# HGRN2 recurrence of a hybrid streaming encoder: keys as logarithms in the exponent, a sigmoid without a reciprocal, merged predicated copies

## The chip, the cores and the metric

The kernel runs on one core of a Trainium2 chip. The metric is the device time of one execution in microseconds (us). Three runs of the kernel before the change gave 1269.4, 1276.73 and 1278.02 us; their median is 1276.73 us.

## The reference

The input x has 2048 tokens of 1024 channels. One layer normalises it, projects it once to 3592 columns, and gives these to three branches whose outputs are gated, joined and projected back. Branch A is the HGRN2 recurrence in four heads of 64 channels, and it is the one that the change touches:

```python
z = f_a
f_gate = lb + (1.0 - lb) * sigmoid(z)
log_f_a = log(maximum(f_gate, TINY))
k_a = (1.0 - lb) * sigmoid(-z)
q = silu(q_a)
...
# by chunk, b = cumsum(log_f) within the chunk, S the 64x64 state of a head
decay = exp(b[t] - b[s]) for s <= t, else 0
attn[t, s] = sum_d q[t, d] * k[s, d] * decay[t, s, d]
o = attn @ v + (q * exp(b)) @ S
S = exp(b_last)[:, None] * S + (k * exp(b_last - b)).T @ v
```

Branch B is a pooling mixer, branch C a forgetting attention with 8 heads. Both need the projections and the attention takes most of the time, but no instruction of theirs changes.

## The kernel before, in words

All matmuls that need more than half precision are done with halves: weights and normalised x are each split in a float16 high and low part, and a projection is three products (24 matmuls of 512 columns for one 128-channel block of 512 tokens). The recurrence itself computes in float32; one float32 matmul stands as two records in the trace.

The work of the recurrence is cut in eight units (g, ct): four groups g of 512 tokens, two blocks ct of 128 channels (two heads, one on partitions 0 to 63, one on 64 to 127). A unit has three pieces.

- hgrn_f projects the forget gate and makes from it, channel by channel, log sigmoid (sg), the key k, the logarithm of the gate (E), its running sum b (a scan on VectorE, L275), and from these the scaled keys and queries: Kd and Qd for the diagonal, khat for the state, qhat for reading the state.
- hgrn_q projects the query and multiplies it with its sigmoid. The sigmoid is 1/(1 + exp(-q)): an Exp on ScalarE (L303), a clamp and an addition (L304) and a reciprocal (L305) on VectorE; the product is qs (L307), which goes into Qd and qhat on GpSimd (VectorE for g = 0).
- hgrn_unit builds the causal 128 x 128 score block of each of four 128-token chunks and two heads in the tile `at`, then multiplies it with the values. The diagonal blocks of two tokens come from pd = Kd.T Qd (L326), one head after the other, masked into `at` by L327. The rest comes in six levels, h = 64, 32, ..., 2: the second half of a block of 2h tokens sees the first half through the value of b at the middle. For each level GpSimd writes two differences into a tile X (L345, L346), ScalarE takes Exp of it (L347), VectorE multiplies the first halves with k (L351) and writes the second halves times qs into a tile Z (L354, once for each head), TensorE makes pl = X.T Z (L358), and VectorE copies pl under a mask into `at`, once for each head (L363). At the second level the states S are carried over the four chunks on VectorE (L378), at the fourth po begins with the state's part (L383), and after the sixth it takes `at` times the values (L390).

The tile X has four buffers, Z three. The eight units follow each other in a loop. In the turn of a unit the features of the next unit (hgrn_f, hgrn_q) are made as well, and the function fill puts other work of TensorE between the levels: projections of the values (L196), of the attention's keys (L185), and the loading and transposing of further x tiles. Each engine has one queue of its own in order; the tile framework decides at build time, by its estimates, in which order the instructions of these pieces stand in each queue. From the last units on, kq_chunk and kq_blocks follow with the attention's projections; they load weights through a staging tile wst with three buffers, split into halves by ScalarE (L163) and VectorE (L166). After the recurrence come the projections, the pooling and the attention.

Of the kernel before, what the change touches and what calls it, by code (L numbers as in the profile page):

```python
# [54 lines left out]
def kernel(  # L55
# [30 lines left out]
    # f_c side: persistent small tables  # L86
# [6 lines left out]
    # DRAM scratch  # L93
# [22 lines left out]
    # normalised x transposed, hi and lo, in two halves of the tokens  # L116
# [61 lines left out]
    def proj_cm(ps, w, c0, g):  # L178
        """channel-major: ps[128 ch, 512 tokens of group g]"""
# [8 lines left out]
    def proj_tm(ps, w, c0, n, t):  # L188
        """token-major: ps[128 tokens of tile t, n channels]"""
# [60 lines left out]
    def hgrn_f(g, ct, wf, bank=None):  # L250
# [10 lines left out]
        # log sigmoid of z and of -z  # L261
# [14 lines left out]
        # blocks of two tokens refer to their first token  # L276
# [10 lines left out]
        G.tensor_tensor(kk.rearrange("p (n t) -> p n t", t=P), bt[:, :, P - 1:P].to_broadcast([P, 4, P]), bt, op=ALU.subtract)  # L287
        S.activation(kk, kk, AF.Exp, bias=0.0, scale=1.0)
        G.tensor_tensor(kk, kk, k, op=ALU.mult)
# [4 lines left out]
        feats[(g, ct)] = dict(k=k, b=b, qd=q_d, kd=k_d, kk=kk, qh=e, el=el)  # L294

    def hgrn_q(g, ct, wq):
# [7 lines left out]
        V.tensor_scalar(th, th, 1e37, 1.0, op0=ALU.min, op1=ALU.add)  # L304
        V.reciprocal(th, th)  # L305
# [10 lines left out]
    def hgrn_unit(g, ct, va):  # L316
        f = feats.pop((g, ct))
        k, b, qs = f["k"], f["b"], f["qs"]
        u = f"_{g}_{ct}"
        at = ap.tile([P, 2, 4, P], F32, tag="at", name=f"at{u}", bufs=2)  # L320
        for hh in range(2):
            r = ds(64 * hh, 64)
            pd = pm(f"pd{u}_{hh}")
            for tt in range(4):
                tok = ds(tt * P, P)
                PE.matmul(pd[:, tok], f["kd"][r, tok], f["qd"][r, tok], start=tt == 0, stop=tt == 3, skip_group_check=True)  # L326
            V.tensor_tensor(at[:, hh], pd.rearrange("p (t s) -> p t s", t=4),  # L327
                            mdiag.unsqueeze(1).to_broadcast([P, 4, P]), op=ALU.mult)
# [6 lines left out]
        # levels of halves: the second half of a block sees its first half through the middle  # L335
        for li, h in enumerate(LEVELS):
# [3 lines left out]
            bv = b.rearrange("p (n two h) -> p n two h", two=2, h=h)  # L340
            Xv = X.rearrange("p (n two h) -> p n two h", two=2, h=h)
# [843 lines left out]
```

## Time and profile before

| | us |
|---|---|
| three runs | 1269.4, 1276.73, 1278.02 |
| median | 1276.73 |
| span of the profiled execution, first to last instruction | 1271.3 |
| median less that span | 5.4 |
| TensorE (PE) busy in the span | 1188.4 |
| VectorE (DVE) busy | 843.6 |
| ScalarE (ACT) busy | 604.2 |
| GpSimd (POOL) busy | 413.5 |

The own time of the profiled execution is not among the files beyond its span; what lies around the span is taken as the 5.4 us that the median has more. The recurrence lies between some 45 us, where the first unit's features are made, and 364 us, where the last unit's output is done.

A busy TensorE is one whose matmul records cover the time; the end of a record is modelled and successive records overlap. "PEclk" is the granted share of its clock. Times of instructions that follow each other on one engine overlap by some tens of nanoseconds too, so a sum of durations is a little more than the time that they cover.

### The profile page before, as it was taken

The numbers are of one execution on the slowest core, as the hardware profiler recorded it, in microseconds if no ns is written. First come the engines' busy times: TensorE is split into PE (matmuls) and PEld (weight loads), VectorE is DVE, ScalarE is ACT, GpSimd is POOL, SyncE is SP. The second block draws the span as 40 slices with busy tenths as digits, with TensorE's granted clock in tenths as the row PEclk, the third lists the DMA queues.
The fourth block names the chain that finished last, engine by engine and source line by source line (L and its number), as shares of the span: only waits on it lengthen the run. The fifth ranks groups of instructions, "written<-read, shape, count | busy, mean of one in ns | idle before, by whom it ended". The sixth has DMA issues, their size and how long they took to land. (4 is left out here: it accounts for less than half of the span.)

```text
span 1271.3 us, 25715 instructions
## 1 busy us (share of the span) xinstructions
PE 1188.4 (93%) x10077; PEld 767.6 (60%) x10077; DVE 843.6 (66%) x1703; ACT 604.2 (48%) x1167; POOL 413.5 (33%) x516
## 2 busy tenths in 40 slices
PE   5878999998999999999999999999999899999998
PEld 3445766655654478885447776765555555555644
DVE  5799888888542244213354798788888898888522
ACT  5745544443221133212122667667667676777611
POOL 2646466554230011001240223234333343334400
PEclk9989999998999999999999999999999999999999
DMA  9636320112146233001012253275222332221253
GB/s 226 165 84 140 77 42 26 43 34 83 47 121 167 77 113 97 11 24 42 18 34 88 77 145 105 63 162 125 81 71 69 85 76 78 48 50 51 70 165 106
DMA packets 168139, 107.57 MB, mean 85 GB/s; under 512 B 95825, under 2 KB 159569, under 8 KB 168017
## 3 DMA queue, kind: packets, MB, share of 16 engines
q1 hardware_dynamic: 166976, 105.92, 31.9%
q8 instruction: 79, 1.29, 0.5%
q14 instruction: 44, 0.35, 0.1%
q10 hardware_dynamic: 1040, 0.00, 0.0%
HBM read 59.62 MB, written 31.59 MB: 72 GB/s over the span
## 5 line engine op out<-in xcount | busy, mean ns | idle before, releaser
L1001 ACT ACTIVATE pf<-st,biasg 128x512 f32<-128x512 f32 (+1 forms) x320 | 199.6, 625 | 101.1 <-PE st L992 59.1
L961 DVE TENSOR_REDUCE M<-mx 128x1 f32<-128x512 f32 (+3 forms) x288 | 173.4, 615 | 18.6 <-PE mx L957 12.0
L196 PEld LDWEIGHTS <-hTh 128*128 128x128 f16 x1536 | 151.1, 99 | 44.9 <-DMA hTh<-xh 15.6
L1006 DVE TENSOR_TENSOR pl<-pf,ph 128x512 f16<-128x512 f32 (+1 forms) x213 | 138.1, 650 | 46.6 <-POOL ph L1003 26.6
L1006 POOL TENSOR_TENSOR pl<-pf,ph 128x512 f16<-128x512 f32 (+2 forms) x107 | 112.7, 1053 | 152.3 <-ACT ph L1005 144.9
L1016 PE MATMUL o<-Vt,ph 128*128 128x65 f16 x1088 | 130.5, 193 | 3.6 <-DVE oc L1030 3.5
L1005 ACT ACTIVATE ph<-st,biasg 128x512 f16<-128x512 f32 (+2 forms) x213 | 131.3, 616 | 1.5 <-PE o L1018 1.5
L1017 PE MATMUL o<-Vt,ph 128*128 128x64 f16 x1088 | 130.9, 195 | 0.0
L1018 PE MATMUL o<-Vt,pl 128*128 128x65 f16 x1088 | 129.8, 192 | 0.0
L1003 POOL TENSOR_SCALAR ph<-pf 128x512 f16<-128x512 f32 (+1 forms) x107 | 65.8, 615 | 195.9 <-ACT pf L1001 124.0
L1016 PEld LDWEIGHTS <-ph 128*128 128x128 f16 x1088 | 103.0, 97 | 35.3 <-DVE oc L1030 5.7
L1017 PEld LDWEIGHTS <-ph 128*128 128x128 f16 x1088 | 102.3, 97 | 24.3 <-issue 0.8
L991 PE MATMUL st<-QQ,K 128*128 128x512 f16 (+1 forms) x320 | 111.4, 348 | 5.1 <-ACT ph L1005 4.3
L1018 PEld LDWEIGHTS <-pl 128*128 128x128 f16 x1088 | 102.7, 99 | 0.4
L1060 PE MATMUL y<-woh,mh 128*128 128x512 f16 (+2 forms) x264 | 98.4, 374 | 0.0
L1060 PE MATMUL y<-woh,ml 128*128 128x512 f16 (+2 forms) x264 | 98.3, 374 | 0.0
L1060 PE MATMUL y<-wol,mh 128*128 128x512 f16 (+2 forms) x264 | 98.3, 374 | 0.0
L957 PE MATMUL mx<-KA,QM 68*128 68x512 f16 (+1 forms) x224 | 79.6, 358 | 4.8 <-DVE M L961 4.0
L196 PEld LDWEIGHTS <-hTl 128*128 128x128 f16 x768 | 76.2, 99 | 10.7
L992 PE MATMUL st<-QB,KA 68*128 68x512 f16 x224 | 80.4, 359 | 0.0
L1060 PEld LDWEIGHTS <-mh 128*128 128x128 f16 x528 | 49.5, 98 | 50.7 <-issue 1.3
L358 PE MATMUL pl<-Z,X 128*128 128x128 f32 x384 | 54.1, 295 | 22.7 <-DVE Z L354 22.7
(327 smaller groups left out, 2738.9 us busy)
## 6 DMA issues: line engine op xcount, KB each, us to landing
xt<-in_x_dram SPq DMA_DIRECT2D x16, 512.0 KB, 4.5
xr<-in_x_dram SPq DMA_DIRECT2D x16, 512.0 KB, 5.0
out_dram<-yt SPq DMA_DIRECT2D x15, 512.0 KB, 3.0
QQ<-qh_d SPq DMA_DIRECT2D x64, 64.0 KB, 2.4
wo<-in_w_out_dram SPq DMA_DIRECT2D x16, 256.0 KB, 3.0
gc_d<-gtc SPq DMA_DIRECT2D x32, 128.0 KB, 2.0
gtl<-gc_d SPq DMA_DIRECT2D x16, 256.0 KB, 3.0
wst_q<-in_w_in_dram SPq DMA_DIRECT2D x12, 256.0 KB, 2.8
```

Of the source, the lines that this page charges most:

```text
L196: PE.matmul(ps, a[:, k, :], b[:, k, c0:c0 + n], start=i == 0, stop=i == 3 * KC - 1)
L957: PE.matmul(mx[:, :w], QMs[i][:68, qi * P:(qi + 1) * P], KA[c][:68, h, :w], start=True, stop=not last)
L961: V.tensor_reduce(dst, mx[:, :w], op=ALU.max, axis=AX.X)
L991: PE.matmul(st[:, off:], K2[c][:, h, jj * P:(jj + 1) * P], QQs[i][:, off:], start=True, stop=False)
L992: PE.matmul(st[:, off:], KA[c][:68, h, jj * P:(jj + 1) * P], QBs[i][:68, off:], start=False, stop=not diag)
L1001: S.activation(pf[:, off:], st[:, off:], AF.Exp, bias=bias, scale=0.125)
L1005: S.activation(ph[:, off:], st[:, off:], AF.Exp, bias=bias, scale=0.125)
L1006: (G if k == 1 else V).tensor_tensor(pl[:, off:], pf[:, off:], ph[:, off:], op=ALU.subtract)
L1016: PE.matmul(pov[:, qi, :], ph[:, qs], Vt[:, j, h, 0:65], start=(j == 0 and qi == 0), stop=False, skip_group_check=True)
L1017: PE.matmul(pov[:, qi, 0:64], ph[:, qs], Vt[:, j, h, 65:129], start=False, stop=False, skip_group_check=True)
L1018: PE.matmul(pov[:, qi, :], pl[:, qs], Vt[:, j, h, 0:65], start=False, stop=(j == 4 * g + qi), skip_group_check=True)
L1060: PE.matmul(py, a[:, k, :], b[:, k, cs], start=i == 0, stop=i == 3 * KC - 1)
```

## The change

The key enters the level's exponent as its logarithm. With log k = log sigmoid(-z) + log(1 - lb), a new tile nb = log k - b is made once for each unit on VectorE (L276 of the changed kernel), and the subtraction of b on the first halves of X becomes an addition of nb, so that the Exp gives the decayed key and the product with k goes. The same is done for khat (the addition of nb on GpSimd, no product) and for Kd (a subtraction of log f from log sigmoid(-z), before the Exp, whose bias is log(1 - lb)). The Exp that gave sigmoid(-z) and the tile k go. The sigmoid of the query becomes exp(-ln(1 + exp(-q))): a clamp on VectorE, then Ln and Exp on ScalarE, in place of the reciprocal. `at` has the chunk ahead of the head in its layout, so that one predicated copy a level serves both heads. The diagonal's matmuls go chunk by chunk, alternating between the heads, into two banks of PSUM. Two small instructions on 128 x 2 elements make log(1 - lb) once.

```diff
@@ hgrn_f
         E1.tensor_tensor(z, sg, z, op=ALU.subtract)
-        S.activation(z, z, AF.Exp, bias=0.0, scale=1.0)
-        k = t512("k", f"k{u}")
-        G.tensor_scalar(k, z, lbt[:, 4 + ct:5 + ct], 1.0, op0=ALU.mult, op1=ALU.mult)
+        lk = lbt[:, 8 + ct:9 + ct]
...
         V.tensor_tensor_scan(b, d0, E, initial=0.0, op0=ALU.mult, op1=ALU.add)
+        nb = t512("nb", f"nb{u}")
+        V.scalar_tensor_tensor(nb, z, lk, b, op0=ALU.add, op1=ALU.subtract)
...
-        S.activation(k_d, lfo, AF.Exp, bias=0.0, scale=-1.0)
+        E1.tensor_tensor(k_d, z, lfo, op=ALU.subtract)
+        S.activation(k_d, k_d, AF.Exp, bias=lk, scale=1.0)
         S.activation(q_d, lfo, AF.Exp, bias=0.0, scale=1.0)
-        E1.tensor_tensor(k_d, k_d, k, op=ALU.mult)
...
-        G.tensor_tensor(kk..., bt[:, :, P - 1:P].to_broadcast([P, 4, P]), bt, op=ALU.subtract)
+        G.tensor_tensor(kk..., bt[:, :, P - 1:P].to_broadcast([P, 4, P]), nb..., op=ALU.add)
         S.activation(kk, kk, AF.Exp, bias=0.0, scale=1.0)
-        G.tensor_tensor(kk, kk, k, op=ALU.mult)
@@ hgrn_q
         S.activation(th, pq, AF.Exp, bias=0.0, scale=-INV)
-        V.tensor_scalar(th, th, 1e37, 1.0, op0=ALU.min, op1=ALU.add)
-        V.reciprocal(th, th)
+        V.tensor_scalar(th, th, 2.0 ** 60, None, op0=ALU.min)
+        S.activation(th, th, AF.Ln, bias=1.0, scale=1.0)
+        S.activation(th, th, AF.Exp, bias=0.0, scale=-1.0)
@@ hgrn_unit
-        at = ap.tile([P, 2, 4, P], F32, tag="at", name=f"at{u}", bufs=2)
-        for hh in range(2):
-            pd = pm(f"pd{u}_{hh}")
-            for tt in range(4):
-                PE.matmul(pd[:, tok], f["kd"][r, tok], f["qd"][r, tok], ...)
+        at = ap.tile([P, 4, 2, P], F32, tag="at", name=f"at{u}", bufs=2)
+        pds = [pm(f"pd{u}_{hh}") for hh in range(2)]
+        for tt in range(4):
+            for hh in range(2):
+                PE.matmul(pds[hh][:, tok], f["kd"][r, tok], f["qd"][r, tok], ...)
...
-            E1.tensor_tensor(Xv[:, :, 0, :], mid, bv[:, :, 0, :], op=ALU.subtract)
+            E1.tensor_tensor(Xv[:, :, 0, :], mid, nbv[:, :, 0, :], op=ALU.add)
             S.activation(X, X, AF.Exp, bias=0.0, scale=1.0)
-            V.tensor_tensor(Xv[:, :, 0, :], Xv[:, :, 0, :], kv[:, :, 0, :], op=ALU.mult)
...
-            for hh in range(2):
-                dst = at[:, hh].rearrange(...)
-                V.copy_predicated(dst, masks[h]....to_broadcast([P, 4, nb, h]), plv[:, :, hh]...)
+            dst = at.rearrange("p t u (n two h) -> p (t u) n two h", two=2, h=h)[:, :, :, 1, :]
+            V.copy_predicated(dst, masks[h]....to_broadcast([P, 8, n2, h]), pl.rearrange("p (u n h) -> p u n h", u=8, h=h))
```

The order of each engine's queue follows from the code and the framework's estimates. On VectorE, in the turn of unit (2, 1) before the change, these rows prepare the next unit (3, 0) and begin the current one; th is the query's sigmoid, el a copy of four columns of qhat:

```order
L273 TENSOR_SCALAR E_0_2338<-E_0_2338,lbt 128x512
L275 SCALAR_TENSOR_TENSOR b_0_2354<-d_391,E_0_2338 128x512
L304 TENSOR_SCALAR th_0_2412<-th_0_2412 128x512
L327 TENSOR_TENSOR at_1_2420<-pd_1_0_2421,mdiag 128x512
L305 RECIPROCAL th_0_2412<-th_0_2412 128x512
L293 COPY el_0_2368<-qhat_0_2366 128x4
L327 TENSOR_TENSOR at_1_2420<-pd_1_1_2427,mdiag 128x512
L307 TENSOR_TENSOR qs_0_2416<-th_0_2412,pq_0_2387 128x512
```

The same place in the changed kernel:

```order
L271 TENSOR_SCALAR E_0_2274<-E_0_2274,lbt 128x512
L273 SCALAR_TENSOR_TENSOR b_0_2287<-d_393,E_0_2274 128x512
L305 TENSOR_SCALAR th_0_2346<-th_0_2346 128x512
L276 SCALAR_TENSOR_TENSOR nb_0_2289<-z_0_2273,lbt,b_0_2287 128x512
L331 TENSOR_TENSOR at_1_2355<-pd_1_0_2356,mdiag 128x4x128
L293 COPY el_0_2302<-qhat_0_2300 128x4
L331 TENSOR_TENSOR at_1_2355<-pd_1_1_2357,mdiag 128x4x128
L309 TENSOR_TENSOR qs_0_2351<-th_0_2346,pq_0_2321 128x512
```

The reciprocal is gone, nb stands where it can run after the scan, and qs, whose input now comes back from ScalarE, stands at the same place. On ScalarE, the same turn before the change has these rows from the query's Exp on:

```order
L303 ACTIVATE th_0_2412<-pq_0_2387 128x512
L282 ACTIVATE Kd_0_2358<-sg_0_2343 128x512
L283 ACTIVATE Qd_0_2357<-sg_0_2343 128x512
L288 ACTIVATE khat_0_2362<-khat_0_2362 128x512
L291 ACTIVATE qhat_0_2366<-b_0_2354 128x512
```

and the changed kernel has these:

```order
L303 ACTIVATE th_0_2346<-pq_0_2321 128x512
L285 ACTIVATE Qd_0_2292<-sg_0_2279 128x512
L291 ACTIVATE qhat_0_2300<-b_0_2287 128x512
L284 ACTIVATE Kd_0_2293<-Kd_0_2293,lbt 128x512
L306 ACTIVATE th_0_2346<-th_0_2346 128x512
L289 ACTIVATE khat_0_2297<-khat_0_2297 128x512
L307 ACTIVATE th_0_2346<-th_0_2346 128x512
```

The Ln and the last Exp of the sigmoid stand behind the Exps of Qd, Kd and khat, whose inputs come from GpSimd. On TensorE, a unit's diagonal before the change (the four matmuls of a head in one row) and the transposes behind it:

```order
L185 MATMUL pq_1_2022<-hTl_102,wh_q 128x512
L326 MATMUL pd_0_0_2056<-Qd_0_1676,Kd_0_1677 128x128 x4
L326 MATMUL pd_0_1_2062<-Qd_0_1676,Kd_0_1677 128x128 x4
L331 MATMUL pk_0_2068<-idf,khat_0_1681 128x128 x4
L196 LDWEIGHTS hTh_101
```

and in the changed kernel:

```order
L185 MATMUL pq_1_1316<-hTl_100,wh_q 128x512
L329 MATMUL pd_0_0_1351<-Qd_0_992,Kd_0_993 128x128
L329 MATMUL pd_0_1_1352<-Qd_0_992,Kd_0_993 128x128
L329 MATMUL pd_0_0_1351<-Qd_0_992,Kd_0_993 128x128
L329 MATMUL pd_0_1_1352<-Qd_0_992,Kd_0_993 128x128
L329 MATMUL pd_0_0_1351<-Qd_0_992,Kd_0_993 128x128
L329 MATMUL pd_0_1_1352<-Qd_0_992,Kd_0_993 128x128
L329 MATMUL pd_0_0_1351<-Qd_0_992,Kd_0_993 128x128
L329 MATMUL pd_0_1_1352<-Qd_0_992,Kd_0_993 128x128
L335 MATMUL pk_0_1363<-idf,khat_0_997 128x128 x4
```

The two heads, on the lower and the upper 64 partitions, alternate; what stands before and behind is the same.

## Rows read from the trace of the kernel before

**Rows 1.** The page: busy us by engine, share of the span, instructions.

```profile
PE 1188.4 (93%) x10077; PEld 767.6 (60%) x10077; DVE 843.6 (66%) x1703; ACT 604.2 (48%) x1167; POOL 413.5 (33%) x516
```

**Rows 2.** Windows from one unit's diagonal to the next: length, busy us, PEclk.

```profile
45.00:62.10 17.10, 16.40 (x100) 9.49 (x98) 15.72 (x20) 13.31 (x25) 12.19 (x20) 1.00 0.38 91
62.10:109.70 47.60, 37.64 (x200) 24.37 (x200) 44.92 (x79) 24.09 (x44) 24.82 (x28) 0.89 0.42 104
109.70:143.50 33.80, 28.60 (x193) 21.82 (x192) 30.25 (x58) 16.75 (x31) 20.11 (x23) 0.90 0.46 96
143.50:181.90 38.40, 34.33 (x245) 26.02 (x244) 32.94 (x58) 19.39 (x37) 24.27 (x26) 0.96 0.29 63
181.90:214.20 32.30, 32.08 (x198) 20.43 (x197) 27.70 (x55) 13.03 (x22) 19.84 (x22) 1.00 0.08 25
214.20:247.20 33.00, 32.47 (x245) 25.04 (x244) 31.24 (x59) 14.57 (x34) 18.18 (x20) 1.00 0.15 41
247.20:282.90 35.70, 32.53 (x197) 20.57 (x196) 31.00 (x60) 16.13 (x30) 21.02 (x23) 1.00 0.10 31
282.90:332.10 49.20, 44.59 (x246) 27.09 (x245) 35.96 (x69) 14.92 (x30) 19.33 (x20) 0.93 0.24 71
332.10:364.50 32.40, 32.40 (x201) 20.81 (x201) 15.61 (x37) 6.12 (x11) 2.44 (x4) 1.00 0.13 43
```

**Rows 3.** Waits, 45 to 366 us: total us, times, longest us.

```profile
POOL X L345 <- PE pl L358: 39.3, 12, 10.3
...
PE pl L358 <- DVE Z L354: 22.7, 11, 5.2
POOL khat L287 <- DVE b L275: 15.8, 4, 8.5
```

**Rows 4.** Timeline around 128 us, DVE then PE: start, us, instruction, idle before.

```profile
124.50 2.46 DVE L378 SCALAR_TENSOR_TENSOR S<-S,el,pu 64x64 f32<-64x64 f32 x8
...
128.35 2.05 PE L358 MATMUL pl<-Z,X 128*128 128x128 f32 x8 [5.20 <-DVE Z L354]
```

**Rows 5.** Groups on DVE, 45 to 366 us: total us, mean ns, idle before.

```profile
L363 DVE COPY_PREDICATED at<-m,pl 128x256 f32<-128x256 int8 x96 | 39.5, 482 | 2.4 <-PE pl L358 2.2
L305 DVE RECIPROCAL th<-th 128x512 f32<-128x512 f32 x8 | 26.7, 3337 | 0.0
L351 DVE TENSOR_TENSOR X<-X,k 128x256 f32<-128x256 f32 x48 | 23.2, 484 | 1.6 <-ACT X L347 0.4
...
L327 DVE TENSOR_TENSOR at<-pd,mdiag 128x512 f32<-128x512 f32 x16 | 10.7, 679 | 0.0
L275 DVE TENSOR_TENSOR_SCAN b<-d,E 128x512 f32<-128x512 f32 x8 | 10.5, 1318 | 0.1
...
L262 DVE SCALAR_TENSOR_TENSOR sg<-z,E 128x512 f32<-128x512 f32 x8 | 5.5, 690 | 4.3 <-ACT E L259 4.2
```

**Rows 6.** Groups on POOL, then on ACT, 45 to 366 us, as above.

```profile
L278 POOL TENSOR_TENSOR sg<-E,odd 128x512 f32<-128x512 f32 x6 | 10.1, 1686 | 10.6 <-DVE E L273 10.6
L287 POOL TENSOR_TENSOR khat<-b 128x512 f32<-128x512 f32 x8 | 9.6, 1196 | 15.8 <-DVE b L275 15.8
...
L284 POOL TENSOR_TENSOR Kd<-Kd,k 128x512 f32<-128x512 f32 x6 | 7.7, 1277 | 0.7 <-ACT Kd L282 0.7
...
L347 ACT ACTIVATE X<-X 128x512 f32<-128x512 f32 x48 | 30.1, 629 | 67.2 <-POOL X L346 63.2 <-DVE at L363 3.0 <-PE pl L358 0.9
```

**Rows 7.** Timeline of PE at 181.9 us and at 189.2 us.

```profile
181.91 1.71 PE L326 MATMUL pd<-Qd,Kd 64*128 64x128 f32 x16
...
189.23 1.95 PE L358 MATMUL pl<-Z,X 128*128 128x128 f32 x16
```

**Rows 8.** Timeline at 300 us, ACT, DVE and PE.

```profile
300.29 0.91 ACT L163 ACTIVATE wh_q<-wst_q,g 128x256 f16<-128x256 f32 x2 [6.97 <-DMA wst_q<-in_w_in_dram]
...
302.66 0.88 DVE L166 SCALAR_TENSOR_TENSOR wl_q<-wst_q,g,wh_q 128x256 f16<-128x256 f32 x2 [0.94 <-ACT wh_q L163]
...
308.92 2.05 PE L358 MATMUL pl<-Z,X 128*128 128x128 f32 x8 [4.61 <-DVE Z L354]
```

More of the change, by code (lines that the diff above doesn't have):

```diff
@@ L293, in hgrn_f @@
         V.tensor_copy(el, e.rearrange("p (n t) -> p n t", t=P)[:, :, P - 1])
-        feats[(g, ct)] = dict(k=k, b=b, qd=q_d, kd=k_d, kk=kk, qh=e, el=el)
+        feats[(g, ct)] = dict(nb=nb, b=b, qd=q_d, kd=k_d, kk=kk, qh=e, el=el)
     def hgrn_q(g, ct, wq):
@@ L317, in hgrn_unit @@
         f = feats.pop((g, ct))
-        k, b, qs = f["k"], f["b"], f["qs"]
+        nb, b, qs = f["nb"], f["b"], f["qs"]
         u = f"_{g}_{ct}"
-        at = ap.tile([P, 2, 4, P], F32, tag="at", name=f"at{u}", bufs=2)
-        for hh in range(2):
-            r = ds(64 * hh, 64)
-            pd = pm(f"pd{u}_{hh}")
-            for tt in range(4):
-                tok = ds(tt * P, P)
-                PE.matmul(pd[:, tok], f["kd"][r, tok], f["qd"][r, tok], start=tt == 0, stop=tt == 3, skip_group_check=True)
-            V.tensor_tensor(at[:, hh], pd.rearrange("p (t s) -> p t s", t=4),
+        at = ap.tile([P, 4, 2, P], F32, tag="at", name=f"at{u}", bufs=2)
+        pds = [pm(f"pd{u}_{hh}") for hh in range(2)]
+        for tt in range(4):
+            tok = ds(tt * P, P)
+            for hh in range(2):
+                r = ds(64 * hh, 64)
+                PE.matmul(pds[hh][:, tok], f["kd"][r, tok], f["qd"][r, tok], start=tt == 0, stop=tt == 3, skip_group_check=True)
+        for hh in range(2):
+            V.tensor_tensor(at[:, :, hh, :], pds[hh].rearrange("p (t s) -> p t s", t=4),
                             mdiag.unsqueeze(1).to_broadcast([P, 4, P]), op=ALU.mult)
@@ L340, in hgrn_unit @@
             bv = b.rearrange("p (n two h) -> p n two h", two=2, h=h)
+            nbv = nb.rearrange("p (n two h) -> p n two h", two=2, h=h)
             Xv = X.rearrange("p (n two h) -> p n two h", two=2, h=h)
@@ L359, in hgrn_unit @@
                           start=tt == 0, stop=tt == 3, skip_group_check=True)
-            nb = 64 // h
-            for hh in range(2):
-                dst = at[:, hh].rearrange("p t (n two h) -> p t n two h", two=2, h=h)[:, :, :, 1, :]
-                V.copy_predicated(dst, masks[h].rearrange("p (n h) -> p n h", h=h).unsqueeze(1).to_broadcast([P, 4, nb, h]),
-                                  plv[:, :, hh].rearrange("p t (n h) -> p t n h", h=h))
+            n2 = 64 // h
+            dst = at.rearrange("p t u (n two h) -> p (t u) n two h", two=2, h=h)[:, :, :, 1, :]
+            V.copy_predicated(dst, masks[h].rearrange("p (n h) -> p n h", h=h).unsqueeze(1).to_broadcast([P, 8, n2, h]),
+                              pl.rearrange("p (u n h) -> p u n h", u=8, h=h))
             if li == 1:
@@ L389, in hgrn_unit @@
                 c = 64 * hh
-                PE.matmul(po[:, tt * P + c:tt * P + c + 64], at[:, hh, tt, :], va[:, tt, ct * P + c:ct * P + c + 64],
+                PE.matmul(po[:, tt * P + c:tt * P + c + 64], at[:, tt, hh, :], va[:, tt, ct * P + c:ct * P + c + 64],
                           start=False, stop=(tt == 3 and hh == 1), skip_group_check=True)
@@ L510 @@
     tok_i(3, wi, toks[0])
-    lbt = ap.tile([P, 8], F32, tag="lbt", name="lbt", bufs=1)
+    lbt = ap.tile([P, 10], F32, tag="lbt", name="lbt", bufs=1)
     nc.sync.dma_start(lbt[:, 0:2], lower_bounds.rearrange("o (c p) -> p (o c)", p=P), allow_slow_non_contiguous=True)
@@ L527 @@
     V.tensor_tensor(lbt[:, 6:8], lb_e, lb_r, op=ALU.add)
+    V.tensor_scalar(lb_e, lbt[:, 4:6], 2.0 ** -50, None, op0=ALU.max)
+    S.activation(lbt[:, 8:10], lb_e, AF.Ln, bias=0.0, scale=1.0)
     wq = load_w([(QA, 256)], "q")
```

3 lines of the change are left out of this document (1 added, 2 removed).

## The prediction

> **What bounds the kernel now.** I read the busy times by engine first. TensorE is busy for 93% of the span, VectorE for 66% [rows 1], so over the whole kernel TensorE is the bound, and a change that takes work from VectorE can win only where TensorE stands idle. The busy share by stage settles where that is. I cut the recurrence at the first diagonal matmul of each unit, so that a window is one turn of its loop [rows 2]; each row gives the window's length, then busy time of PE, weight load, DVE, ACT and POOL, and the granted clock. The reader is to subtract: in nine windows of 319.5 us together, TensorE is busy for 291.0, so 28.5 us of idle time is all that lies there. It sits in the second (10.0), third (5.2), fourth (4.1), seventh (3.2) and eighth (4.6) window and is 0.7 or less in the others. After 332 us TensorE is covered to the last digit. In the second window VectorE is busy for 44.9 of 47.6 us: there VectorE is the bound. In the third, fourth and seventh it has 87 to 90%, close enough that its queue comes late in bursts.
>
> The clock adds something. The granted share is 0.89, 0.90, 0.96 and 0.93 in the four windows with the longest idle stretches and 1.00 elsewhere [rows 2]: in them TensorE fell to 1.2 GHz of its 2.4 after it had stood idle. The missing share times the length is 5.2 + 3.4 + 1.5 + 3.4 = 13.5 us of clock, most of it under work, so some 10 us of work was done late for that.
>
> Then the waits: TensorE's largest wait in this stretch is the first level matmul behind Z, 22.7 us in 11 waits [rows 3]. The timeline shows one such wait, of 5.2 us, with VectorE working all the while: state updates for 2.46 us, then copies, then Z [rows 4]. So most of the idle time is VectorE's queue being late with Z, and VectorE is what the change relieves.
>
> **The change part by part**, for one unit and VectorE first.
>
> - The reciprocal goes: 3.34 us [rows 5].
> - Six products with k go, 6 x 0.484 = 2.9 us [rows 5].
> - Twelve masked copies of 256 columns, 12 x 0.482 = 5.8 us, become six of 512. No row shows such a copy with 512. Not more than two of the old, 0.96; not less than the masked product of 512 columns from PSUM, 0.68 [rows 5], so six cost 4.1 to 5.8 us. A masked copy of 256 costs about what a product of 256 costs, 0.48, so I take near the middle, 5.2: a gain of 0.6.
> - nb is new: a scalar_tensor_tensor on 128 x 512, 0.69 us by its sister on L262 [rows 5].
> - The clamp remains as one instruction on the same tile; the two instructions on 128 x 2 elements come once and are hidden under the weights' split at the start; at worst their cost is a fraction of a us.
>
> Sum: 3.34 + 2.9 + 0.6 - 0.69 = 6.15 us less on VectorE for each unit, 49 us over eight. GpSimd loses a product of 1.3 to 1.4 us and the scaling of k for each unit, and its remaining instructions keep their number; it is at most 63% busy in these windows [rows 2] and hides what it does. ScalarE loses one Exp and gains a Ln and an Exp, 0.63 us net by the Exp of the same size [rows 6]; it is at half load.
>
> A new wait comes with it. The order shows qs at the same place in VectorE's queue, but its sigmoid now ends on ScalarE behind the Exps of Kd and khat, which wait for GpSimd. From E on, GpSimd needs 1.69 + 1.28 + 1.20 = 4.2 us for sg, Kd and khat, and two Exps follow at 0.63 [rows 6]: qs can start about 5.4 us after E. VectorE has the scan, nb, two products for the diagonal, the clamp and el ahead, 1.32 + 0.69 + 2 x 0.68 and about 0.6: 4.0 us [rows 5]. So VectorE stands some 1.5 us at qs, with the masked copies, the state updates and Z of the running unit queued behind it, and TensorE waits for that Z. This may be nothing where E is late anyway, and up to the reciprocal's own 3.3 us where GpSimd is held; I take 1.5 where VectorE bounds, which leaves 4.6 us of a turn.
>
> Diagonal: 16 records take 1.71 us now; 16 records of the level matmuls, which use all 128 partitions, take 1.95 [rows 7]. So the two heads already run side by side for a little, 0.24 us, at the one place where they meet. Alternating can bring between nothing and the time of eight records, 1.71 - 0.98 = 0.7 us a unit. I take 0.4, in the seven windows in which TensorE will be the bound: 2.8 us.
>
> The Trainium skill's page "TensorE: Matmul & The Clock Gate", section "Part 3: Packing small matmuls — row/col tiling", says that matmuls on different row groups of the array run concurrently, at nearly the time of one. By that rule the gain is the whole 0.7 us a unit, 5.6 over eight, and the total would be 3 us below mine; the trace shows only the partial overlap just named.
>
> Now the windows. A window can't be shorter than TensorE's work at full clock, nor than VectorE's.
>
> - First: 0.7 idle, 0.5 of it gained.
> - Second: VectorE bounds before and after, about 40 us against TensorE's 37.6 less the clock's part; it gives the 4.6 of VectorE and about 0.9 because the first b comes before a reciprocal instead of behind it: 5.5.
> - Third: VectorE falls from 30.2 to about 25.6, TensorE has 28.6 with 0.10 of the clock missing, about 26.9; with some waiting left, 29.0 of 33.8: 4.8.
> - Fourth: TensorE about 33 at full clock, VectorE 28; 34.0 of 38.4: 4.4.
> - Fifth and sixth: TensorE is already the bound; 0.4 of 0.75.
> - Seventh: 3.2 idle, VectorE down to 26 of 35.7: 2.3.
> - Eighth: here the late Z hangs on weights as well. ScalarE waits 6.97 us for a weight transfer and VectorE then for ScalarE, before the 4.61 us in which TensorE stands [rows 8]. The transfer starts when VectorE has freed a staging buffer, so it comes earlier by the reciprocal but keeps its own length: half of the 4.6 + 3.4 of idle and clock, 4.0.
> - Ninth: nothing.
>
> Sum: 0.5 + 5.5 + 4.8 + 4.4 + 0.4 + 2.3 + 4.0 = 21.9, with the diagonal 24.7 us. The profiled span of 1271.3 becomes 1246.6. The median of the runs is 5.4 above that span, which I keep: 1276.7 - 24.7 = 1252.0 us. What follows the recurrence stays in order and simply starts earlier, since TensorE has no idle time there in which to lose the gain.
>
> **Rivals.**
>
> 1. TensorE alone bounds. All 28.5 us of idle time, the 10 of the clock and the 2.8 go: 1276.7 - 41.3 = 1235.4. For it: VectorE ends at least 2 us below TensorE in every window but the second. Against it: the second, and the weights in the eighth. Chance 0.17.
> 2. The sigmoid's new way takes the reciprocal's place: VectorE stands at qs for about the 3.3 us that it saves, and only the products and copies, 2.8 us less a unit, count. That is half: 1276.7 - 12.5 = 1264. For it speaks ScalarE's new order, against it that in four windows VectorE has time to stand. Chance 0.13.
> 3. The levels are bound elsewhere, and VectorE was only the last in a chain: ScalarE waits 63.2 us for GpSimd's X [rows 6], GpSimd 39.3 us for TensorE to free X [rows 3]. Then only the shorter chain inside the waits and the diagonal remain, some 4 us: 1273. Against it: GpSimd has a third of each window free. Chance 0.12.
> 4. Slower: VectorE's stop at qs becomes longer than the 6.15 us saved. The place is the turn of each unit, where khat on GpSimd stands behind X of the running unit, X behind TensorE's pl, and pl behind a Z that is queued behind qs. GpSimd's longest waits of this kind are 10.3 us for pl and 8.5 for khat's b [rows 3]. At 8.5 a unit the kernel loses 8 x (8.5 - 6.15) = 19 us: 1296. It decides from 6.15 us of stop on; my estimate is 1.5. Chance 0.08.
>
> The Trainium skill speaks for the fourth in "TensorE: Matmul & The Clock Gate", section "Architectural detail: the array is 16× 32×32, not 1× 128×128": VectorE's and ScalarE's queues are strictly first in, first out, so nothing overtakes a waiting qs. By that rule, the trace agrees: copies and state updates follow VectorE's wait for weights at 302.66 us [rows 8].
>
> **How the numbers follow.** The forecast has a chance of 0.50, with 1245 to 1259 as its own range: 7 us either way for the stop at qs between nothing and 3.3, the copies between 4.1 and 5.8, and the diagonal between nothing and 0.7. With the rivals' 0.17 below, 0.13 and 0.12 above and 0.08 slower, the range of 8 in 10 is 1233 to 1268. A change of over 1% is about 12.8 us, and that is about what a measurement of this kernel tells from none: below 1264 faster, above 1289.5 slower. Faster: 0.50 + 0.17 + nearly three quarters of rival 2, 0.09: 0.76. Same: the rest of rival 2, rival 3 and the mildest of rival 4: 0.18. Slower: 0.06.
>
> **What would show it.** In the changed profile VectorE should be busy some 45 us less up to 364 us, with no reciprocal of 512 columns and 48 masked copies of about 0.87 us. TensorE's waits for Z should fall from 22.7 us to under 10, mostly in the first unit and the last two. VectorE should show a wait for th from ScalarE of 1 to 2 us a unit; 6 us or more there proves the fourth rival, none the first. The diagonal should take about 1.3 us. The last recurrence output should leave some 25 us earlier and the later stages keep their length; if those lengthen, the forecast is wrong in what it left out.

## The result, and the profile after

The changed kernel takes 1258.42 us, the median of four runs from 1256.87 to 1260.66; four runs of the kernel before beside it had a median of 1275.82. The ratio is 0.987, with a 95% interval of 0.9846 to 0.9895: faster by 17.4 us, where the prediction had 24.7. The profiled execution has a span of 1256.6 us and took 1258.33, so 1.7 us lie outside its span; in the runs below it is 1.6 to 2.1. The 5.4 us that stand for this before the change must then be for the most part the distance of a quicker execution from the median. The two spans differ by 14.7 us (1271.3 to 1256.6), and the windows below account for these 14.7, not for the 17.4 of the medians. On its page VectorE is busy 32.1 us less than in [rows 1] (843.6 to 811.5), not 45 less.

The page of the changed kernel, busy us by engine:

```profile
PE 1177.0 (94%) x10077; PEld 758.5 (60%) x10077; DVE 811.5 (65%) x1608; ACT 608.9 (48%) x1176; POOL 398.3 (32%) x500
```

The windows of the changed kernel, cut as in [rows 2] at each unit's first diagonal matmul: length, then busy us of PE, weight load, DVE, ACT and POOL, granted clock, DMA share, GB/s. The last window runs to the end of the last output, which in the kernel before is at 368.4 us.

```profile
45.00:62.20 17.20, 17.20 (x105) 9.94 (x103) 16.04 (x23) 13.24 (x25) 15.56 (x26) 1.00 0.26 64
62.20:106.70 44.50, 36.06 (x198) 22.72 (x197) 36.50 (x60) 24.64 (x45) 15.41 (x19) 0.88 0.49 130
106.70:145.00 38.30, 28.60 (x197) 21.63 (x196) 29.54 (x52) 22.78 (x40) 21.87 (x24) 0.91 0.53 131
145.00:178.65 33.65, 31.97 (x245) 24.48 (x244) 24.46 (x43) 15.39 (x31) 20.38 (x21) 1.00 0.03 9
178.65:210.55 31.90, 31.49 (x197) 19.95 (x196) 25.52 (x43) 13.65 (x23) 18.00 (x19) 1.00 0.08 25
210.55:242.30 31.75, 31.75 (x247) 24.42 (x246) 27.24 (x49) 17.20 (x37) 18.66 (x19) 1.00 0.16 43
242.30:274.20 31.90, 31.50 (x199) 19.94 (x198) 27.20 (x46) 15.42 (x29) 17.18 (x19) 1.00 0.12 34
274.20:319.90 45.70, 43.66 (x245) 25.58 (x244) 31.97 (x56) 16.14 (x31) 18.29 (x19) 0.96 0.27 76
319.90:355.90 36.00, 36.00 (x219) 22.20 (x219) 17.00 (x35) 8.72 (x17) 5.48 (x7) 1.00 0.19 58
```

Set against [rows 2], the second window is 3.1 us shorter, the third 4.5 *longer*, the fourth 4.7 shorter, the seventh 3.8 and the eighth 3.5. The last output of the recurrence leaves 12.5 us earlier (368.4 to 355.9), and what follows it takes 900.8 us instead of 902.9.

One caution on such numbers: the time after the recurrence is the same code in every kernel of this study, and in fourteen profiles it lies between 899.2 and 906.1 us. Two or three microseconds of a single profile's span are no evidence. The medians are, and so are some windows: the sixth and the ninth repeat to 0.3 us in kernels that don't touch them. The seventh does so with the change, but takes 35.6 to 37.3 us in kernels without it that don't touch it.

Waits of the changed kernel, 45 to 356 us (total us, times, longest):

```profile
PE pl L361 <- DVE Z L357: 15.0, 6, 8.4
...
PE pu L370 <- ACT khT L337: 7.6, 3, 4.6
...
DVE xl L222 <- ACT xh L220: 7.1, 5, 1.8
...
ACT xh L215 <- DMA xt<-in_x_dram: 4.9, 2, 3.2
...
DVE ss L216 <- ACT xh L215: 4.0, 2, 3.1
...
DVE qs L309 <- ACT th L307: 1.8, 3, 0.6
```

The wait for Z of [rows 3] fell from 22.7 only to 15.0 us, more than half of it in one piece of 8.4. The stop at qs, which the prediction put at 1.5 us a unit, is 1.8 us in all eight units. A wait for khT, the transposed keys that ScalarE copies from PSUM, is new. New as well are waits for the x tiles (xt, xh, xl and ss belong to the normalisation of x, of which eight tiles pass through these windows): VectorE stands 7.1 + 4.0 us for ScalarE's part of them, and ScalarE 4.9 us for the loading of x. In the kernel before, from 55 to 366 us, VectorE stood 1.3 us for a tile and ScalarE not at all for a load:

```profile
DVE xl L222 <- ACT xh L220: 1.3, 2, 1.0
```

Groups on VectorE in the changed kernel, 45 to 356 us, as [rows 5]:

```profile
L357 DVE TENSOR_TENSOR Z<-X,qs 64x256 f32<-64x256 f32 x96 | 51.6, 537 | 1.5
L365 DVE COPY_PREDICATED at<-m,pl 128x512 f32<-128x512 int8 x48 | 38.7, 806 | 1.3 <-PE pl L361 1.1
...
L273 DVE TENSOR_TENSOR_SCAN b<-d,E 128x512 f32<-128x512 f32 x8 | 12.0, 1498 | 0.1
...
L276 DVE SCALAR_TENSOR_TENSOR nb<-z,lbt,b 128x512 f32<-128x512 f32 x8 | 10.5, 1307 | 0.0
```

nb costs 1.31 us, not 0.69. The 48 merged copies keep VectorE busy for 38.7 us, where the 96 of [rows 5] did for 39.5: the merge saved almost nothing. And the scan costs 1.50 instead of 1.32.

### The profile page after: what moved, and what is told of

The parts are those of the page before. It is cut to its first block, busy times and chain, and to the rows that moved or that the text cites. A ratio compares the mean times of both kernels' runs of the same rounds, so it can differ in the third digit from the quotient of the medians.

```text
span 1256.6 us, 25632 instructions
## 1 busy us (share of the span) xinstructions
PE 1177.0 (94%) x10077; PEld 758.5 (60%) x10077; DVE 811.5 (65%) x1608; ACT 608.9 (48%) x1176; POOL 398.3 (32%) x500
## 3 DMA queue, kind: packets, MB, share of 16 engines
q1 hardware_dynamic: 166976, 105.92, 32.1%
## 5 line engine op out<-in xcount | busy, mean ns | idle before, releaser
L196 PEld LDWEIGHTS <-hTh 128*128 128x128 f16 x1536 | 150.6, 99 | 46.4 <-DMA hTh<-xh 18.6
L196 PE MATMUL pgc<-wh_gc,hTh 128*128 128x256 f16 x256 | 67.3, 275 | 1.2 <-DVE gtb L848 1.2
```

The source lines that it names most:

```text
L196: PE.matmul(ps, a[:, k, :], b[:, k, c0:c0 + n], start=i == 0, stop=i == 3 * KC - 1)
```

## The experiments

Twelve kernels ran, in three sets. "Windows" are cut as above, and each ratio is to runs of the kernel before on the same chip.

### First set: which part pays

Theory A: relief of VectorE is worth about what it takes off, except in the first units, which the x tiles and the khT copy hold. Theory B: the sigmoid on ScalarE gave back what the reciprocal's removal won.

**Keys as logarithms alone.** The kernel before with the edit's key half, and sigmoid, copies and diagonal as they were:

```diff
-        S.activation(z, z, AF.Exp, bias=0.0, scale=1.0)
...
-        G.tensor_scalar(k, z, lbt[:, 4 + ct:5 + ct], 1.0, op0=ALU.mult, op1=ALU.mult)
...
+        V.scalar_tensor_tensor(nb, z, lk, b, op0=ALU.add, op1=ALU.subtract)
...
-            V.tensor_tensor(Xv[:, :, 0, :], Xv[:, :, 0, :], kv[:, :, 0, :], op=ALU.mult)
```

> Only the keys as logarithms, all else as before. Theory A (VectorE relief is worth what it takes off, and the first two units are held by the x tiles' chain): VectorE loses 6 products of 0.48 us and gains nb for each unit, about 2.2 us net, so the units from the third on gain about 5 us together: ratio about 0.995. Theory B (the sigmoid on ScalarE is what ate the expected gain): the keys alone bring most of the measured gain, ratio 0.988 or lower.

Measured: 1273.65 us, ratio 0.9991 [0.9973, 1.0009]. No gain: neither theory A's 0.5% nor theory B's 1.2%.

**The sigmoid alone.**

```diff
-        V.tensor_scalar(th, th, 1e37, 1.0, op0=ALU.min, op1=ALU.add)
-        V.reciprocal(th, th)
+        V.tensor_scalar(th, th, 2.0 ** 60, None, op0=ALU.min)
+        S.activation(th, th, AF.Ln, bias=1.0, scale=1.0)
+        S.activation(th, th, AF.Exp, bias=0.0, scale=-1.0)
```

> Only the query's sigmoid by Ln and Exp in place of the reciprocal. Theory A: 3.3 us less on VectorE for each unit, worth 6 to 8 us from the third unit on: ratio about 0.995, with the copy khT to ScalarE late in the first unit by a few us. Theory B: the waits at qs and khT eat it, ratio 1.000 or above.

Measured: 1261.98 us, ratio 0.99 [0.9876, 0.9924], a gain of some 13 us, about twice what theory A expected. Theory B falls here.

**Copies and diagonal alone.**

```diff
-            for tt in range(4):
-                tok = ds(tt * P, P)
-                PE.matmul(pd[:, tok], f["kd"][r, tok], f["qd"][r, tok], start=tt == 0, stop=tt == 3, skip_group_check=True)
+        for tt in range(4):
+            tok = ds(tt * P, P)
+            for hh in range(2):
+                r = ds(64 * hh, 64)
+                PE.matmul(pds[hh][:, tok], f["kd"][r, tok], f["qd"][r, tok], start=tt == 0, stop=tt == 3, skip_group_check=True)
...
-                V.copy_predicated(dst, masks[h].rearrange("p (n h) -> p n h", h=h).unsqueeze(1).to_broadcast([P, 4, nb, h]),
-                                  plv[:, :, hh].rearrange("p t (n h) -> p t n h", h=h))
+            V.copy_predicated(dst, masks[h].rearrange("p (n h) -> p n h", h=h).unsqueeze(1).to_broadcast([P, 8, n2, h]),
+                              pl.rearrange("p (u n h) -> p u n h", u=8, h=h))
```

> Only the merged copies and the diagonal with alternating heads. Both theories: the diagonal takes 1.16 us instead of 1.71, so 8 x 0.55 = 4.4 us where TensorE bounds; the copies save 0.16 us each on VectorE: ratio about 0.997.

Measured: 1278.39 us, ratio 1.0036 [1.0019, 1.0054], slower, where both theories had a gain, though the diagonal takes 1.16 us a unit instead of 1.71.

**The change with the reciprocal put back.**

```diff
-        S.activation(th, th, AF.Ln, bias=1.0, scale=1.0)
-        S.activation(th, th, AF.Exp, bias=0.0, scale=-1.0)
+        V.reciprocal(th, th)
```

> The change with the reciprocal put back. Theory A: VectorE is 3.3 us busier for each unit, of which TensorE covers a part: 1262 to 1266 us, ratio to before about 0.991. Theory B: no wait for the sigmoid on ScalarE, ratio 0.985 or lower, below the change's 0.987.

Measured: 1265.35 us, ratio 0.9928 [0.9901, 0.9955]. Of the change's gain some 7 us go with the reciprocal's return. What remains, keys with copies and diagonal, is more than their product alone, 0.9991 x 1.0036; so the parts depend on each other, and this part of it stays open.

The sigmoid is the largest part, and to take the products with k away, 2.9 us a unit in the prediction's sum, is worth nothing by itself. The timelines show a reason in the fifth window, where no x tile is near. The rows follow VectorE's queue from sg of the next unit's features to the first Z of the running unit behind these features, first in the kernel before:

```profile
177.41 0.69 DVE L262 SCALAR_TENSOR_TENSOR sg<-z,E 128x512 f32<-128x512 f32 x1 [0.76 <-ACT E L259]
...
186.29 3.33 DVE L305 RECIPROCAL th<-th 128x512 f32<-128x512 f32 x1
...
195.13 1.18 DVE L354 TENSOR_TENSOR Z<-X,qs 64x256 f32<-64x256 f32 x2
```

then with the keys alone:

```profile
179.92 0.69 DVE L262 SCALAR_TENSOR_TENSOR sg<-z,E 128x512 f32<-128x512 f32 x1 [4.38 <-ACT E L259]
...
188.19 1.76 DVE L276 SCALAR_TENSOR_TENSOR nb<-z,lbt,b 128x512 f32<-128x512 f32 x1
...
199.32 0.76 DVE L353 TENSOR_TENSOR Z<-X,qs 64x256 f32<-64x256 f32 x1
...
205.04 1.13 PE L357 MATMUL pl<-Z,X 128*128 128x128 f32 x8 [1.25 <-DVE Z L353]
```

and in the changed kernel, with further places of its timeline that the text below uses:

```profile
74.64 2.07 PE L370 MATMUL pu<-va,khT 128*128 128x128 f32 x8 [4.59 <-ACT khT L337]
...
79.57 0.75 DVE L276 SCALAR_TENSOR_TENSOR nb<-z,lbt,b 128x512 f32<-128x512 f32 x1
...
100.26 0.84 DVE L357 TENSOR_TENSOR Z<-X,qs 64x256 f32<-64x256 f32 x2
102.30 1.28 DVE L222 SCALAR_TENSOR_TENSOR xl<-xt,ss,xh 128x1024 f16<-128x1024 f32 x1 [1.19 <-ACT xh L220]
...
105.49 1.28 DVE L222 SCALAR_TENSOR_TENSOR xl<-xt,ss,xh 128x1024 f16<-128x1024 f32 x1 [1.84 <-ACT xh L220]
...
113.49 1.28 DVE L222 SCALAR_TENSOR_TENSOR xl<-xt,ss,xh 128x1024 f16<-128x1024 f32 x1 [1.00 <-ACT xh L220]
...
123.15 1.28 DVE L222 SCALAR_TENSOR_TENSOR xl<-xt,ss,xh 128x1024 f16<-128x1024 f32 x1 [1.20 <-ACT xh L220]
...
125.03 0.81 DVE L357 TENSOR_TENSOR Z<-X,qs 64x256 f32<-64x256 f32 x1
...
127.38 2.05 PE L361 MATMUL pl<-Z,X 128*128 128x128 f32 x8 [8.41 <-DVE Z L357]
...
174.14 0.69 DVE L262 SCALAR_TENSOR_TENSOR sg<-z,E 128x512 f32<-128x512 f32 x1 [4.43 <-ACT E L259]
...
178.65 1.16 PE L329 MATMUL pd<-Qd,Kd 64*128 64x128 f32 x16
...
182.42 1.76 DVE L276 SCALAR_TENSOR_TENSOR nb<-z,lbt,b 128x512 f32<-128x512 f32 x1
...
188.72 1.35 DVE L357 TENSOR_TENSOR Z<-X,qs 64x256 f32<-64x256 f32 x1
...
192.96 1.31 DVE L357 TENSOR_TENSOR Z<-X,qs 64x256 f32<-64x256 f32 x3
```

The path from sg to Z is 17.7 us before (177.41 to 195.13) and 19.4 with the keys alone. The reciprocal stands on it with its 3.33 us, and nb stands on it too, with 1.76. The products with k do not: they lay between the levels, where TensorE had other matmuls to do. So the keys put work on the path and took work off beside it, and TensorE, which stands 0.2 us in the fifth window before, stands 1.25 us for a Z at 205.04. In the changed kernel the path is cut in another way: one half of that Z comes ahead of the state updates, 14.6 us after sg, the other half behind them at 192.96, 18.8 us after it, and sg itself had waited 4.43 us for ScalarE.

That fits the missing gain in this window; no run moved nb off the path. Over all windows, cut as above, the keys alone gain 2.7 us in the second, 1.0 in the seventh and 2.1 in the eighth, and lose 4.4 in the third and fourth, where the x tiles pass, 2.0 in the fifth and sixth and 0.8 ahead of the first diagonal. "No gain" is a sum of gains and losses of one profile each, and why each came is not shown.

### Second set: x tiles, and the parts' company

Theory X: the windows of the first units gained nothing because the x tiles stand in the features' queues there. Rival K: the features' own chain and khT set them. The edit for the next two is the same; it leaves out the loading of tiles 8 to 15 with the rest of their work, and tells what the tiles cost, not which part of them:

```diff
+        kept[:] = xh, xl
...
     def x_load(xpool, t, tag="xt"):
+        if t >= 8:
+            hh, hl = h_at(t * P, P)
+            nc.sync.dma_start_transpose(hh, kept[0])
+            nc.sync.dma_start_transpose(hl, kept[1])
+            return
```

**The kernel before without the work on tiles 8 to 15.**

> The kernel before, in which tiles 8 to 15 of x are not loaded, scaled and split inside the recurrence; the transposing DMAs of their two halves remain, from the halves of tile 7. This leaves out the normalisation of half of x. It is the base for the run beside it. Theory X (in the windows of the first two units the change brought nothing because the x tiles' work on ScalarE, VectorE and GpSimd, one behind the other in the queues of the features, sets their length): windows two and three of before, 47.7 + 33.8 us, lose a few us only, because VectorE's own work sets them here: 76 to 80 us, and the whole lies near 1268. Rival K (the features' own chain and the copy of khat set these windows): 80 us or more, 1270 to 1274.

**The changed kernel without it.**

> The changed kernel with the same work on x left out. Theory X: the gain predicted for windows two and three appears once the x tiles are gone: together 68 to 72 us (they take 82.8 in the changed kernel), TensorE's idle time there falls from 18.1 to under 8 us, and the distance to the kernel before with the same work left out is 22 to 28 us. Rival K: the windows stay at 78 to 82 us and the distance stays at 14 to 18 us.

Measured: 1264.18 us, ratio 0.9933 [0.991, 0.9956], and 1245.58 us, ratio 0.9788 [0.9764, 0.9813]. The second to fourth windows of the first of them:

```profile
62.20:109.80 47.60, 37.21 (x196) 24.81 (x196) 42.47 (x75) 17.76 (x33) 22.42 (x25) 0.86 0.51 107
109.80:139.60 29.80, 27.37 (x198) 20.34 (x197) 27.41 (x53) 12.64 (x24) 19.69 (x22) 1.00 0.04 10
139.60:172.60 33.00, 32.45 (x245) 25.04 (x244) 28.80 (x53) 13.44 (x28) 19.98 (x22) 1.00 0.03 9
```

and of the second:

```profile
60.60:105.60 45.00, 36.18 (x199) 22.38 (x198) 34.92 (x57) 19.22 (x37) 16.15 (x17) 0.85 0.66 140
105.60:134.80 29.20, 27.19 (x197) 19.90 (x196) 24.37 (x41) 13.25 (x25) 18.58 (x19) 1.00 0.04 10
134.80:166.50 31.70, 31.70 (x245) 24.42 (x244) 24.16 (x41) 14.04 (x29) 18.43 (x19) 1.00 0.04 10
```

Half of each theory stands, and neither had the first time, which lies below the 1268 of theory X and the 1270 to 1274 of rival K. The x tiles do make the idle time of the third and fourth windows: without them the kernel before needs 29.8 and 33.0 us there instead of 33.8 and 38.4, with the reciprocal and all products still in place, and the clock stays at 1.00. But they cost the changed kernel about as much (38.3 + 33.65 to 29.2 + 31.7, 11.1 us against 9.4), so they don't explain what the change failed to gain: the distance between the two is 18.6 us without them and 17.4 with them, not the 22 to 28 of theory X. The second window does not shrink in either.

**Keys and sigmoid without copies and diagonal.** The change with `V.copy_predicated` in two pieces and the loop over heads outside the tiles, as the kernel before has them.

> The change without its copies and its diagonal: keys as logarithms and the sigmoid without a reciprocal, masked copies of 256 columns and the diagonal one head after the other as before. If the parts add, as ratios, 0.9991 x 0.99 = 0.989, 1261.5 us. If copies and diagonal cost by themselves what they cost alone (0.4%), this is faster than the changed kernel: 1253 to 1255. If they pay only once VectorE is relieved, it is slower than the changed kernel: 1262 to 1266, with the diagonal 0.55 us a unit longer in the five units that TensorE bounds.

Measured: 1259.59 us, ratio 0.9891 [0.9866, 0.9915]: exactly the product 0.9991 x 0.99. Copies and diagonal then add 0.2% in the whole change, which the intervals don't separate from nothing.

**The alternating diagonal alone.** The first half of the diff of copies and diagonal.

> The kernel before with the alternating diagonal alone. The diagonal falls from 1.71 to 1.16 us a unit; TensorE bounds five units, so 2.7 us at most come off: 1272.7. If the 0.4% that copies and diagonal together cost came from here (the product with the mask can start only when both heads are done, and two banks are held at once), it is 1278 to 1280 and the single merged copy is free of it; if it came from the merged copy (a wait for a level's all four tiles, 0.8 us in one piece ahead of Z), this is 1272 to 1275.

Measured: 1273.09 us, ratio 1.0 [0.9982, 1.0017]. By difference the 0.4% that the pair costs alone come with the merged copy, not with the diagonal; the copy alone was not run, and the two intervals almost touch. One part of it is in the traces: in the run of the pair the copies took 0.9 us less than before (38.6 for 39.5), but the 96 Z between them 3.5 us more (51.0 for 47.5; 48.2 with the diagonal alone).

### Third set: the order in the queues

Both edits pin instructions of ScalarE behind its copy of khT in some unit: `behind` adds an edge that sets the order in the queue and adds no wait. Nothing is left out.

**khT first in the first unit** (theory Q: order sets the second window; rival V: VectorE's chain does).

```diff
+        if (g, ct) == (0, 1):
+            behind(i_, (0, 0))
...
+        if t in (8, 9):
+            behind(i_, (0, 0))
```

The first two lines stand behind the second Exp of the features and behind the query's first Exp, the last two behind the square of an x tile.

> The changed kernel, complete, in which ScalarE makes the first unit's khT before the second Exp of the next unit's features, its query's Exp and the squares of tiles 8 and 9, and not behind them. Theory Q (in the window of the first unit TensorE loses time because instructions wait in the wrong order in ScalarE's queue, not because VectorE has too much to do): the state update's matmuls no longer stand 4.6 us for khT, the second window falls from 44.5 to 40 to 41.5 us, and the whole is 3 to 5 us faster: 1253.5 to 1255.5. Rival V (VectorE's work sets that window, 36.5 us of it busy and the rest waits of its own chain): the next Z is late by as much, the window stays at 43.5 to 45 us and the whole within 1 us of the changed kernel.

Measured: 1257.38 us, ratio 0.9864 [0.9828, 0.9899]; the second window is 43.5 us. The matmuls of that window on TensorE's timeline:

```profile
71.03 1.13 PE L382 MATMUL pu<-va,khT 128*128 128x128 f32 x8 [1.64 <-ACT E L276]
84.79 1.13 PE L373 MATMUL pl<-Z,X 128*128 128x128 f32 x8 [4.18 <-DVE Z L369]
```

The state update's wait of 4.59 us shrank to 1.64, for an Exp that the edit put behind khT and no longer for khT itself, and the next wait for Z grew from 1.25 to 4.18 us. Idle time in the window is 8.4 us in both, and the window is 1.0 us shorter, inside what rival V expected. Rival V holds: VectorE's chain sets this window, and most of a wait removed ahead of it is paid behind it.

**Tiles 12 to 15 later.**

```diff
+        if t >= 12:
+            behind(i_, (1, (t - 12) // 2))
```

> The changed kernel, complete, in which the squares of x tiles 12 and 13 go on ScalarE behind khT of the third unit, and those of 14 and 15 behind khT of the fourth. Theory X: the third window (38.3 us) loses what x tiles 12 and 13 cost the next unit's features there, 5 to 8 us, down towards the 29.3 us that it takes without any x tile; the fourth to sixth windows, with TensorE as bound, take the tiles in at 1 to 2 us: 1251 to 1254. Rival: the tiles cost as much wherever they stand, the fourth and fifth windows grow by as much as the third shrinks, and the time is 1257 to 1260.

Measured: 1266.71 us, ratio 0.9942 [0.9923, 0.9962], 0.7% or some 9 us slower than the changed kernel by the two ratios, and slower than both expectations. Its third to fifth windows:

```profile
108.20:140.30 32.10, 27.56 (x199) 20.01 (x198) 25.86 (x45) 14.59 (x27) 21.37 (x21) 1.00 0.20 52
140.30:182.10 41.80, 34.48 (x247) 26.52 (x246) 26.61 (x45) 18.17 (x35) 20.57 (x21) 0.88 0.21 57
182.10:220.20 38.10, 33.96 (x197) 22.45 (x196) 27.00 (x47) 17.68 (x29) 19.57 (x21) 0.91 0.19 49
```

The third window fell from 38.3 to 32.1 as expected. The fourth and fifth grew by 8.2 and 6.2, although VectorE is busy for only 26.6 of 41.8 us there. The timeline in the fourth:

```profile
151.04 0.15 DVE L224 TENSOR_SCALAR ss<-ss 128x1 f32<-128x1 f32 x1 [1.22 <-ACT xh L221]
151.39 1.08 POOL L227 TENSOR_TENSOR ss<-ss,cneg 128x1 f32<-128x1 f32 x2
151.97 2.19 ACT L228 ACTIVATE xh<-xt,ss 128x1024 f16<-128x1024 f32 x2 [0.96 <-POOL ss L227]
...
153.15 3.33 DVE L230 SCALAR_TENSOR_TENSOR xl<-xt,ss,xh 128x1024 f16<-128x1024 f32 x2 [1.95 <-ACT xh L228]
...
161.10 2.05 PE L369 MATMUL pl<-Z,X 128*128 128x128 f32 x8 [7.32 <-DVE Z L365]
```

A tile goes from ScalarE (sum of squares) to VectorE, GpSimd (power), ScalarE (xh) and back to VectorE (xl). VectorE stood 1.22 and 1.95 us for it, then spent 3.33, with Z behind all that in its queue.

**Both orders.**

> The changed kernel with both orders. If they are separate, the gains add: 1246 to 1250, and the cumulated gain at the fourth unit's diagonal, negative at the third unit's in the changed kernel, is what the prediction had there, some 15 us. If the first order only hands the third window more work, the gain is that of the second order alone, 1251 to 1254.

**Both orders in the kernel before.**

> The kernel before with both orders: the squares of tiles 12 to 15 and, in the first unit, the features' Exp of z, the query's Exp and the squares of tiles 8 and 9 go behind khT. Theory X: before has the x tiles' cost in the third and fourth windows (with the tiles left out they lose 4.0 and 5.4 us), so it gains 5 to 9 us from the second order: 1265 to 1270; VectorE's reciprocal and products still hold its second window at 46 to 48 us. The change is then worth 18 to 22 us under the same order. Rival: it gains as much as the changed kernel or more, and the change stays worth 17 us or less under the same order; then VectorE's relief was never worth what I took it for.

Measured: 1263.1 us, ratio 0.9919 [0.9889, 0.9948], and 1281.51 us, ratio 1.0056 [1.0034, 1.0078]. Later tiles cost both kernels, where every expectation for the two had a gain over the kernel without the orders. The distance between the two is 18.4 us: the change is worth the same 17 to 19 us with the tiles as they were, without them, and in an order that is bad for both; each of these distances is good to some 4 us. No kernel that computes the whole is faster than the changed kernel by more than its interval. Whether tiles one at a time, between two levels, or loaded earlier, would cost less was not tried.

## Why the prediction was right, and where it was not

**The bound.** That TensorE bounds outside the windows with idle time, and that only idle time can be won, holds: the fifth to ninth windows took 186.5 us before (32.3 + 33.0 + 35.7 + 49.2 + 36.3, the ninth to the last output) and 177.25 after, 9.2 us less. The terms for them were 0.4 + 2.3 + 4.0 and five diagonals at 0.4, 8.7 us.

**The failing step** is the reading of the third and fourth windows, "VectorE falls from 30.2 to about 25.6 ... 4.8" and "34.0 of 38.4: 4.4": it lets a window shrink with VectorE's busy time. Together with their diagonals the two were to give 10 us. They gave 0.2 (72.2 to 71.95): the fourth took 4.7 and the third gave back 4.5. VectorE's busy time in the two did fall nearly as forecast, from 63.2 to 54.0 us. But what fell there became waiting: its idle time grew from 9.0 to 18.0 us.

In the kernel before, VectorE was late with the Z of [rows 4] because it was full, from 111.08 us on without a pause: with the next unit's features and their reciprocal, with copies, and with the last step of an x tile.

```profile
113.42 3.35 DVE L305 RECIPROCAL th<-th 128x512 f32<-128x512 f32 x1
...
120.74 1.77 DVE L222 SCALAR_TENSOR_TENSOR xl<-xt,ss,xh 128x1024 f16<-128x1024 f32 x1
```

By the run without them the x tiles cost the kernel before 9.4 us over the two windows, nearly all of their idle and clock time, with the reciprocal still in place; and they are no part of the change. In the changed kernel VectorE comes to the tiles before they are ready: its waits for them, 1.3 us before, are 11.1 now (7.1 + 4.0). The prediction has no term for this wait. The profile before had a sign of the tiles: read back from the late Z, VectorE's queue holds their xl, five of 1.6 us in the two windows. That the waits would take the place of the work could not be read there. VectorE's 87 to 90% of a window, as the prediction has it (the fourth has 86), was no bound.

In the changed kernel the tiles fell together in the third window: it has four xl and the fourth window none, where the kernel before had two and three. Between the Z at 100.26 and the one at 125.03 VectorE makes four xl of 1.28 us and stands 5.2 us ahead of them for xh (1.19 + 1.84 + 1.00 + 1.20), and TensorE stands 8.41 us behind it. The Trainium skill's page "TensorE: Matmul & The Clock Gate", section "Architectural detail: the array is 16× 32×32, not 1× 128×128", has the queues of VectorE and ScalarE strictly first in, first out; the trace agrees, Z at 125.03 follows the xl of 123.15 although its own X and qs were there earlier. The first of these tiles was itself late: VectorE had stood 3.08 us for its square ahead of the Z at 100.26, and ScalarE 3.17 us for its load. With the tiles ordered later, the loss went along with them, to the fourth and fifth windows. That the tiles cost as much in each of the orders that ran is shown; which part of a tile, its load or its way through the engines, costs it is open.

**The second window** was to give 5.5 us and gave 3.1. VectorE did lose 8.4 us of work there (44.92 to 36.50). But TensorE's three waits (2.60, 4.59 and 1.25 us) all end by 87.42 us, and up to 97 us VectorE has one pause of 0.98 us and one of 0.26: it is still full where TensorE waits for it. The run with khT first agrees.

**Sizes on VectorE.** The sum was 6.15 us a unit; the page has 32.1 us in eight units, 4.0. The reciprocal (3.34) and the six products (2.9) went as priced. nb was mis-sized, 1.31 for 0.69, and the copies gained 0.1 instead of 0.6. The mean of 0.81 us was inside the bounds, but two old copies ran partly over each other, so the old pair cost 0.82 by busy time (39.5 over 48), not 0.96. Z went from 47.5 to 51.6 us over the same 96 instructions, the scan from 10.5 to 12.0 over eight.

**The stop at qs** was estimated at 1.5 us a unit, and is 0.2. nb and other work keep VectorE until th is there.

**The diagonal** was taken at 0.4 and is 0.55 us a unit (1.71 to 1.16 for the same 16 records, [rows 7]). The Trainium skill's page "TensorE: Matmul & The Clock Gate", section "Part 3: Packing small matmuls — row/col tiling", has row groups run at nearly the time of one; the trace agrees nearly, 1.16 against the 0.98 of eight records. But by the run of the diagonal alone it is worth nothing that can be measured, 1.0 [0.9982, 1.0017].

**The eighth window** was to give 4.0 and gave 3.5.

**Rivals.** TensorE alone as bound did not come: some 23 us of its idle time are left in the recurrence (310.90 less 288.23 in the windows above). The prediction's sign for this rival, no stop at qs, was nearly there (0.2 us a unit), so the sign was wrong. The sigmoid taking the reciprocal's place is refuted by the run of the sigmoid alone, the slower case by the 1.8 us at qs. The third rival, levels bound elsewhere with VectorE last in a chain, was the nearest in kind, for the third and fourth windows; what it named (GpSimd's X) was not the cause.

**The sum** therefore came out at the right sign and inside the range for a mixed reason: the reciprocal paid, as the mechanism says, and 10 us were promised from idle time that the x tiles hold. Part of it is luck. The span was to be 1246.6 us and is 1256.6, 10.0 us too long; 3.7 of these were made up by the 5.4 us added to the span, which are 1.7. The signs that the prediction gave missed with it: VectorE 32 us less busy for 45, waits for Z of 15.0 for under 10, the last output 12.5 us earlier for 25.

## What to carry to other kernels

Price a removed instruction by where it stands: on the path from one late result to the next it can count, between instructions that another engine covers it counts nothing. Even on the path it need not count in full: eight reciprocals are 26.7 us, and their removal alone brought some 13. Ahead of a late instruction, read what its queue holds back to the first wait, and ask whether that is work the change touches, and whether its inputs would be there if the queue came to it earlier. If a stage's idle time comes from other work passing through the same queues, leave that work out in a run, in the kernel before as well as after, to learn how much of the idle time can be won at all.

## What the runs showed of the hardware

- The same instruction, nb on 128 x 512, took 0.75 us at 79.57 and 1.76 us at 182.42. In the first case GpSimd stood waiting for nb until it ended; in the second it ran Kd, a subtraction on 128 x 512, at the same time (182.29 to 183.62). A price on VectorE read where GpSimd is idle can be less than half of the price beside it.
- A masked copy of 512 columns costs 0.81 us in the mean, and a pair of 256 columns 0.82 by busy time: merging saved an instruction but hardly any time.
- Two 64-partition matmul streams in alternation take 1.16 us for 16 records, where one stream after the other takes 1.71.
- TensorE's granted clock was under 1.00 in windows with long waits and 1.00 in covered ones: 0.88 in the changed kernel's second window (8.4 us idle), 1.00 in its fifth (0.4 us). The sum of the idle time doesn't settle it: with the tiles later, the third window had 4.5 us of it in several waits and 1.00, the fifth 4.1 us, all in one wait, and 0.91.
